# Spreading row norm factors through DRAM by two DMAs in a two-mixer decoder

## The chip, the cores and the metric

The kernel runs on one core of one Trainium2 chip. The metric is the device time of one execution in microseconds (us); lower is better. The profile is of one execution, taken by the hardware profiler.

## The reference

Two decoder layers work on 528 tokens (16 learned ones and the sequence of 512) with 1024 channels. Each layer is a half-step SwiGLU, a mixer and another half-step SwiGLU; layer 0 mixes by retention, layer 1 by gated linear attention (GLA), each with four heads. Both mixers end in the same way, and the change lies there:

```python
def rmsnorm(x, g):
    y = x * lax.rsqrt(jnp.mean(x * x, axis=-1, keepdims=True) + EPS)
    return y * g

# retention: 4 heads of 512 values     # gla: 4 heads of 256 values
o = rmsnorm(from_chunks(o), head_norm)
o = o.reshape(b, T, HEADS * DV) * jax.nn.silu(g)
return o @ w_out
```

So each token has, in each head, one factor 1/sqrt(mean square + EPS), by which all of the head's values are multiplied.

## The kernel before

**Layout.** Activations lie with channels on the partitions and tokens along the free axis. A retention head's output is four tiles of 128 x 528, a GLA head's two of 128 x 512 (the 16 learned tokens aren't needed any more there). A token's mean square is therefore a sum over partitions and tiles, and its factor must then stand on all 128 partitions.

**Products.** Every float32 product is three (`mm3`, L398 to L400): the high part of the weights by the high part of the data, the low by the high, the high by the low. A weight tile is loaded by a DMA into `raw` or `pair`, ScalarE casts it to its high half (`whi`, L159), and VectorE subtracts for the low half (`wlo`, L160). Projections go in "units", a 2 x 2 scheme of block products with seven steps (a11, s1, s2, a12, s3, s4, a22). A step of `rqk` (q or k of a retention head) is 12 products of 128 x 264. The steps sum into the PSUM tiles X and QZ; the results are put together by VectorE and ScalarE (for q and k: `row1` L1124, `c22` L1127, `c21` L1130), the first into tile 0, the others into tile 1 of `rtq` or `rtk`. The last step, a22, adds into X again and so has to wait until c22 has read X.

**What sets the order.** Each engine runs its own instructions in the order in which the scheduler put them, and that follows the program's order with some steps marked as urgent. After every step of a unit `hook` prepares further weights and counts down a queue of small jobs, `later(n, fn)`: the job at the head runs after n hooks. So the norm's parts are laid between steps of the next head's q and k units.

**The norm factors** (`rsqrt_rows`, L434). ScalarE squares the head's tiles and VectorE adds them up into `osq` (GLA: `gs`). TensorE multiplies each column block of 88 (GLA: 128) tokens, as weights, by one column of ones: `st`, with tokens on the partitions and a column per block (L443). VectorE scales it (`ms`, L446), GpSimd raises it to the power -1/2 (`r`, L448). VectorE multiplies `r` into blocks of the identity (`dg`, L450), and TensorE multiplies ones by `dg` (L456), which puts each token's factor on all partitions, in the PSUM tile `bc`: two products of 264 for a retention head, one of 512 for a GLA head. Each of these is float32, without the split in three. Then `finish` runs: in retention VectorE multiplies (L1335, half-width, eight of them), ScalarE casts the high part `ogh` (L431) and VectorE subtracts for the low part `ogl` (L432).

**Around the change.** In retention, head h's q unit, rotation (L1136 to L1145, `raq`, `rbq`, `rtq`, and the results `q`) and k unit are followed by `out(h - 1)`, the output projection of the head before (`po_r`), which reads `ogh` and `ogl`; values (`Xrv`), scores, gates (`gs0` to `gs3`) and the head's own products (`po`) come after. In GLA the heads are worked in pairs p = 0, 1 with j = 0, 1; the fourth's sums stand beside the output projection of the first pair. Behind head (1, 0) four tiles of the residual, spilled to DRAM earlier, are loaded again on SyncE's queue (L1937, 528 KB each).

Of the kernel before, what the change touches and what calls it, by code (L numbers as in the profile page):

```python
# [217 lines left out]
def trunk(ctx, tc, a):  # L218
# [163 lines left out]
    def later(n, fn):  # L382
        pend.append([n, fn])
# [50 lines left out]
    def rsqrt_rows(sq, parts, width, name, finish):  # L434


        n = sq.shape[1]
        np_ = n // parts
        w = 88 if n % 264 == 0 else 128
        nj = n // w  # L440
        st = bank(f"st_{name}")
        for j in range(nj):
            nc.tensor.matmul(st[:w, j:j + 1], lhsT=sq[:, j * w:(j + 1) * w], rhs=ones[:, 0:1],  # L443
                             start=(j == 0), stop=(j == nj - 1), skip_group_check=True)
# [3 lines left out]
        G.tensor_tensor(r[:w, :nj], ms[:w, :nj], half_neg[:w, :nj], ALU.pow)  # L448
        dg = tmp.tile([P, T], F32, tag="hf", name=f"dg_{name}")
        V.tensor_tensor(dg[:w, :n].rearrange("p (j t) -> p j t", j=nj),  # L450
                        ident[:w, :w].unsqueeze(1).broadcast_to([w, nj, w]),
                        r[:w, :nj].unsqueeze(2).broadcast_to([w, nj, w]), ALU.mult)

        def spread(q):
            bc = bank(f"bc_{name}{q}")
            nc.tensor.matmul(bc[:, :np_], lhsT=ones[:w, :], rhs=dg[:w, q * np_:(q + 1) * np_], start=True, stop=True)  # L456
            finish(bc, q)

        return [lambda q=q: spread(q) for q in range(parts)]

    def enter(gcol, by, lag=1, lag2=1):

# [90 lines left out]
    def pair(t, halves):  # L553

        return t[:, halves[0][0]:halves[1][1]].rearrange("p (b t) -> p b t", b=2)
# [516 lines left out]
    def retention(feed):  # L1072
        with tc.tile_pool(name="retp", bufs=1) as rp, tc.tile_pool(name="wmore", bufs=2) as wp, psum_pool(4) as pp:
# [40 lines left out]
            def head(h):  # L1114
                qk = {}

                def rope_pair(s):


                    t = [(rp if s == "k" else tmp).tile([P, T], F32, tag=f"gs{m}" if s == "k" else "sg",  # L1120
                                                        name=f"rt{s}{h}{m}") for m in range(2)]

                    def row1(ab, qz):
                        V.tensor_add(pair(t[0], HALVES), ab, qz)  # L1124

                    def c22(c, s_):
                        V.tensor_add(t[1][:, b0:b1], c, s_)  # L1127

                    def c21(c):
                        S.copy(t[1][:, a0:a1], c)  # L1130
# [189 lines left out]
                if h < RH - 1:  # L1320
# [20 lines left out]

# [31 lines left out]
    def gla(feed):  # L1373
        with tc.tile_pool(name="glap", bufs=1) as gp, psum_pool(2) as pp, \
# [448 lines left out]
            def pv(p, j):  # L1823
# [11 lines left out]
                            n == 0, False)  # L1835
                    nc.tensor.matmul(po[:, m, :], lhsT=vh[:3 * MR, 0, c], rhs=pr["PM"][:, j, :], start=False, stop=True)
# [4 lines left out]
                S.activation(s1[:, :512], po[:, 0, :], AF.Square)  # L1841
# [6 lines left out]
                def fin(bc, _):  # L1848
                    for m in range(2):
                        t = tmp.tile([P, 528], F32, tag="hf", name=f"gt{h}{m}")  # L1850
                        V.tensor_mul(t[:, :512], ob[:, m, :], bc)
# [8 lines left out]
                        split(oh[:, NM:], ol[:, NM:], t[:, :512])  # L1860
                        pr["og"][j, m] = (oh, ol)

                pr.setdefault("og", {})
                return lambda: rsqrt_rows(s1[:, :512], 1, 256, f"go{h}", fin)[0]

            def run(steps):
                for st in steps:
# [45 lines left out]
            renorm()  # L1913

            other["banks"], other["ring"] = 0, collections.deque(("bank0",))
            st = pv(0, 0)
            run(g[-n:4 - n])
            sp = st()
            run(g[4 - n:])
            sp()  # L1920
# [12 lines left out]
            sp = st()  # L1933
            run(g[n + 4:])
            for k in range(4):
                xs[k] = stream(k)
                nc.sync.dma_start(xs[k], spilt[k])  # L1937
            x[:] = [xs[d % 4][:, d // 4, :] for d in range(KD)]
            sp()
            st = pv(1, 1)  # L1940
            other["banks"], other["ring"] = 2, collections.deque(("bank0", "bank1"))
            out_step(0)
            sp = st()
            out_step(1)
            sp()
            out_step(2)
            out_step(3)
# [99 lines left out]
```

## Time and profile before

| | us |
|---|---|
| median of 3 runs | 2074.59 (2074.48 to 2075.45) |
| the profiled execution: span | 2072.5 |
| TensorE busy | 2061.5 (99%) |
| VectorE busy | 1789.9 (86%) |
| ScalarE busy | 1192.8 (58%) |
| GpSimd busy | 209.3 (10%) |

The span runs from the first to the last instruction of the profiled execution. Matmuls are pipelined, so that the start of one less the start of the one before, and not its own duration, says what it occupies. In rows of the timeline the columns are start, duration, engine, line, operation, output and inputs, shapes, and how many records are grouped; at the end may stand the idle time before and what ended it. Float32 products show two records each, with one weight load each.

### The profile page before, as it was taken

What the parts mean: (1) busy time and instruction counts of PE and PEld (TensorE: products, weight loads), DVE (VectorE), ACT (ScalarE), POOL (GpSimd) and SP (SyncE); (2) the same over time, 40 slices, a digit from 0 to 9 for tenths busy, and PEclk for the clock granted to TensorE, in tenths of its full rate; (3) what the DMA queues carried; (4) which work ended last, traced back from release to release, by engine and by line L of the source; (5) the groups of instructions that cost most, each with busy time, mean ns of one, the idle gap of its engine ahead of it and who ended that gap; (6) DMA issues with size and microseconds to landing.
All of it is one profiled execution on the core that took longest, in us unless ns stands there. A gap on an engine that the chain in (4) does not pass through costs nothing. (4 is left out here: it accounts for less than half of the span.)

```text
span 2072.5 us, 42971 instructions
## 1 busy us (share of the span) xinstructions
PE 2061.5 (99%) x16367; PEld 2016.6 (97%) x16367; DVE 1789.9 (86%) x3214; ACT 1192.8 (58%) x2330; POOL 209.3 (10%) x181
## 2 busy tenths in 40 slices
PE   9999999999999999999999999999999999999998
PEld 9999999999999999999999999999999988999998
DVE  8989889968686879988889998889997968998886
ACT  5656566554545455656566565666655445666664
POOL 1011111010101000111111011110101000111110
PEclk9999999999999999999999999999999999999999
DMA  7676767354554531776776376676614341686762
GB/s 223 159 190 162 193 179 193 98 144 132 144 133 131 142 101 67 183 188 161 187 194 179 107 180 181 151 208 172 200 57 117 93 162 60 166 210 175 183 178 72
DMA packets 176111, 318.84 MB, mean 154 GB/s; under 512 B 17568, under 2 KB 40736, under 8 KB 175904
## 3 DMA queue, kind: packets, MB, share of 16 engines
q1 hardware_dynamic: 133856, 237.04, 34.0%
q0 software_dynamic: 40896, 75.51, 22.4%
q10 hardware_dynamic: 1152, 3.55, 0.5%
q8 instruction: 128, 2.10, 0.4%
q14 instruction: 79, 0.65, 0.1%
HBM read 311.76 MB, written 4.26 MB: 152 GB/s over the span
## 5 line engine op out<-in xcount | busy, mean ns | idle before, releaser
L159 ACT CAST whi<-raw 128x512 fp32r<-128x512 f32 (+1 forms) x893 | 526.0, 606 | 484.3 <-DVE raw L165 97.3
L160 DVE TENSOR_TENSOR wlo<-raw,whi 128x512 fp32r<-128x512 f32 (+1 forms) x893 | 583.8, 669 | 143.4 <-ACT whi L159 136.1
L159 ACT CAST whi<-pair 128x512 fp32r<-128x512 f32 (+1 forms) x304 | 183.5, 604 | 119.5 <-PE Xf11u L399 7.3
L160 DVE TENSOR_TENSOR wlo<-pair,whi 128x512 fp32r<-128x512 f32 (+1 forms) x304 | 202.0, 665 | 7.0 <-ACT whi L159 5.6
L128 POOL DMA_DIRECT2D pair<-in_f_in x73 | 88.5, 1213 | 720.7 <-DVE wlo L160 338.7
L165 DVE TENSOR_TENSOR raw<-pair,raw 128x512 f32<-128x512 f32 (+1 forms) x146 | 97.3, 667 | 2.6
L167 DVE TENSOR_TENSOR raw<-raw,raw 128x512 f32<-128x512 f32 (+1 forms) x146 | 97.2, 666 | 2.4
L128 POOL DMA_DIRECT2D pair<-in_f_out x44 | 53.2, 1208 | 380.4 <-DVE wlo L160 133.6
L399 PE MATMUL po_r<-ogl,whi 128*128 128x264 f32 x256 | 72.7, 284 | 0.0
L398 PE MATMUL po_r<-ogh,whi 128*128 128x264 f32 x256 | 72.6, 283 | 0.0
L400 PE MATMUL po_r<-ogh,wlo 128*128 128x264 f32 x256 | 72.5, 283 | 0.0
L128 POOL DMA_DIRECT2D pair<-in_ret_in x20 | 24.3, 1216 | 297.2 <-DVE wlo L160 144.3
L398 PE MATMUL Xf20o<-hf,whi 128*128 128x264 f32 x176 | 50.9, 289 | 0.2
L398 PE MATMUL Xf11o<-hf,whi 128*128 128x264 f32 x176 | 50.9, 289 | 0.2
L398 PE MATMUL Xf10o<-hf,whi 128*128 128x264 f32 x176 | 50.8, 289 | 0.2
L399 PE MATMUL Xf10o<-hf,whi 128*128 128x264 f32 x176 | 50.0, 284 | 0.0
L399 PE MATMUL Xf11o<-hf,whi 128*128 128x264 f32 x176 | 50.0, 284 | 0.0
L399 PE MATMUL Xf20o<-hf,whi 128*128 128x264 f32 x176 | 50.0, 284 | 0.0
L400 PE MATMUL Xf20o<-hf,wlo 128*128 128x264 f32 x176 | 49.9, 285 | 0.0
L400 PE MATMUL Xf11o<-hf,wlo 128*128 128x264 f32 x176 | 49.9, 285 | 0.0
L400 PE MATMUL Xf10o<-hf,wlo 128*128 128x264 f32 x176 | 49.9, 285 | 0.0
L400 PEld LDWEIGHTS po_r<-ogh,wlo 128*128 128x128 f32 x256 | 48.2, 188 | 0.0
(987 smaller groups left out, 8523.9 us busy)
## 6 DMA issues: line engine op xcount, KB each, us to landing
raw<-in_f_in SPq DMA_DIRECT2D x277, 256.0 KB, 4.4
pair<-in_f_in SPq DMA_DIRECT2D x150, 256.0 KB, 4.7
pair<-in_f_in POOLq DMA_DIRECT2D x73, 512.0 KB, 6.4
raw<-in_f_out SPq DMA_DIRECT2D x80, 256.0 KB, 3.7
raw<-in_ret_in SPq DMA_DIRECT2D x76, 256.0 KB, 3.0
raw<-in_f_out SPq DMA_DIRECT2D x72, 192.0 KB, 3.0
pair<-in_f_out SPq DMA_DIRECT2D x48, 256.0 KB, 3.8
pair<-in_f_out POOLq DMA_DIRECT2D x24, 512.0 KB, 5.8
```

The costliest lines, as they stand in the source:

```text
L128: nc.gpsimd.dma_start(t, aps[2].unsqueeze(1).broadcast_to([P, 2, n]), accum_op=ALU.add)
L159: self.nc.scalar.copy(hi[:, :n], raw)
L160: V.tensor_sub(lo[:, :n], raw, hi[:, :n].bitcast(F32))
L165: V.tensor_add(s2, self.tiles[c][:, 1], self.tiles[c, "a11"])
L167: V.tensor_add(raw, raw, s2)
L398: nc.tensor.matmul(ps, lhsT=lh, rhs=rh, start=start, stop=False, **kw)
L399: nc.tensor.matmul(ps, lhsT=lh, rhs=rl, start=False, stop=False, **kw)
L400: return nc.tensor.matmul(ps, lhsT=ll, rhs=rh, start=False, stop=stop, **kw)
```

## The change

Retention heads 0, 1, 2 and all four GLA heads use a new function `rsqrt_sent`; retention head 3 and the norms between the blocks keep `rsqrt_rows`. The new function is four steps that the caller spaces out with `in_turn`:

- stats: the column sums as before, but the columns of one product are every sixth (GLA: fourth) token, so that the factors of consecutive tokens lie side by side on a partition; then scaling and power as before.
- send: a DMA on ScalarE's queue writes the 88 x 6 (GLA: 128 x 4) factors to a row in DRAM.
- fetch: a DMA on the same queue reads this row for each of the 128 partitions into an SBUF tile: the tile of the sums (`osq`, `gs1`) itself, or for the first head of a GLA pair a tile of its own, `gbc`.
- finish: the products with the factors, now full-width and in place (`gs0` to `gs3`, `gob`), and the split.

The tiles of k's rotation, which share buffers with the gate tiles, are now claimed when first written. The diff, cut to its core:

```diff
+    rows = ctx.enter_context(tc.tile_pool(name="rows", bufs=2, space=bass.MemoryType.DRAM))
...
+    def rsqrt_sent(sq, width, name, finish, into=None):
+        n = sq.shape[1]
+        w = 88 if n % 264 == 0 else P
+        nj = n // w
+        row = rows.tile([w, nj], F32, tag="row", name=f"row_{name}")
...
+                nc.tensor.matmul(st[:w, j:j + 1], lhsT=sq.rearrange("p (r j) -> p j r", j=nj)[:, j, :], rhs=ones[:, 0:1],
+                                 start=(j == 0), stop=(j == nj - 1), skip_group_check=True)
...
+        def send():
+            nc.scalar.dma_start(row, hold["r"][:w, :nj])
+
+        def fetch():
+            hold["bc"] = into() if into else sq
+            nc.scalar.dma_start(hold["bc"], row.rearrange("r j -> (r j)").unsqueeze(0).broadcast_to([P, n]))
+
+        return stats, send, fetch, lambda: finish(hold["bc"])
...
                     def row1(ab, qz):
-                        V.tensor_add(pair(t[0], HALVES), ab, qz)
+                        V.tensor_add(pair(place(0), HALVES), ab, qz)
...
-                    def fin(bc, q0, q1):
+                    def fin(bc):
                         for m in range(4):
-                            t = tmp.tile([P, T], F32, tag="hf", name=f"og{h}{m}{q0}")[:, :q1 - q0]
-                            V.tensor_mul(t, sgs[m][:, q0:q1], bc[:, :q1 - q0])
-                            split(og[h][0][m][:, q0:q1], og[h][1][m][:, q0:q1], t)
-
-                    later(2, lambda: stats(sqs, fin))
+                            V.tensor_mul(sgs[m], sgs[m], bc)
+                            split(og[h][0][m], og[h][1][m], sgs[m])
+
+                    in_turn((2, 2, 2, 3), rsqrt_sent(sqs, RDV, f"ro{h}", fin))
...
-                ob = gp.tile([P, 2, 512], F32, tag="Pd", name=f"gob{h}")
+                ob = gp.tile([P, 2, 512], F32, tag="Pd" if j else "Q", name=f"gob{h}")
...
-                        V.tensor_mul(t[:, :512], ob[:, m, :], bc)
+                        V.tensor_mul(ob[:, m, :], ob[:, m, :], bc)
...
+                return rsqrt_sent(s1[:, :512], 256, f"go{h}", fin, None if j else into)
...
-            st = pv(0, 1)
-            later(3, lambda st=st: later(3, st()))
+            fetch()
+            chain = pv(0, 1)
+            fin()
+            in_turn((3, 2, 2, 3), chain)
...
-            st = pv(1, 0)
+            stats, send, fetch, fin = pv(1, 0)
             run(g[n:n + 4])
-            sp = st()
-            run(g[n + 4:])
+            stats()
+            run(g[n + 4:n + 6])
+            send()
+            run(g[n + 6:])
+            fetch()
...
+            chain = pv(1, 1)
+            fin()
+            in_turn((1, 1, 1, 2), chain)
```

Lines of the changed kernel stand a little lower: L398 to L400 become L399 to L401, L1124 and L1127 become L1165 and L1168, L1136 to L1145 become L1177 to L1186; the head products are L1375, send and fetch L482 and L486. The scheduler's order changes with it, as the next pieces show (numbers behind names count tiles).

VectorE, in retention's second head, while its k unit runs and the first head is finished. Before, the head products (`og`, from `bc_ro`) and their low parts (`ogl`) stand around k's combine (`rtk11`), with q's rotation behind them:

```order
L432 TENSOR_TENSOR ogl0_6071<-og00264_6244,ogh0_6070 128x264
L160 TENSOR_TENSOR wlo274_6352<-raw138_6145,whi274_6351 128x512
L1127 TENSOR_TENSOR rtk11_6278<-Xrqkk1_6279,surqkk1_6281 128x264
L432 TENSOR_TENSOR ogl0_6071<-og01264_6248,ogh0_6070 128x264
L1335 TENSOR_TENSOR og02264_6252<-gs02_5834,bc_ro01_6242 128x264
L1335 TENSOR_TENSOR og03264_6256<-gs03_5835,bc_ro01_6242 128x264
L1124 TENSOR_TENSOR rtk10_6277<-surqkk1_6281,QZrqkk1_6280 128x528
L432 TENSOR_TENSOR ogl0_6071<-og02264_6252,ogh0_6070 128x264
L432 TENSOR_TENSOR ogl0_6071<-og03264_6256,ogh0_6070 128x264
L1136 TENSOR_TENSOR raq1_6261<-rtq10_6076,ropeq1_6072 128x528
L1138 TENSOR_TENSOR rbq1_6262<-rtq11_6077,ropeq1_6072 128x528
L1137 TENSOR_TENSOR rtq10_6076<-rtq10_6076,ropeq1_6072 128x528
```

The same place in the changed order:

```order
L1185 TENSOR_TENSOR rtq10_6203<-rtq10_6203,rtq11_6182 128x528
L1186 TENSOR_TENSOR q10_1_6235<-raq1_6228,q00_1_6234 128x528
L1375 TENSOR_TENSOR gs00_5699<-gs00_5699,osq0_5973 128x528
L433 TENSOR_TENSOR q11_1_6237<-rtq10_6203,q01_1_6236 128x528
L1375 TENSOR_TENSOR gs01_5700<-gs01_5700,osq0_5973 128x528
L433 TENSOR_TENSOR ogl0_6073<-gs00_5699,ogh0_6072 128x528
L1375 TENSOR_TENSOR gs02_5836<-gs02_5836,osq0_5973 128x528
L1165 TENSOR_TENSOR rtk10_6372<-surqkk1_6246,QZrqkk1_6245 128x528
L433 TENSOR_TENSOR ogl0_6073<-gs01_5700,ogh0_6072 128x528
L433 TENSOR_TENSOR ogl0_6073<-gs02_5836,ogh0_6072 128x528
L1168 TENSOR_TENSOR rtk11_6352<-Xrqkk1_6244,surqkk1_6246 128x264
L1375 TENSOR_TENSOR gs03_5837<-gs03_5837,osq0_5973 128x528
```

q's rotation has moved ahead of the head products, and k's combine `rtk11` behind most of them and behind `rtk10`.

TensorE at the end of the same k unit. Before, a22 into `Xrqkk1` ends and the out-projection `po_r00` begins:

```order
L400 MATMUL Xrqkk1_6279<-rth_4954,wlo269_6196 128x264
L398 MATMUL Xrqkk1_6279<-rth_4954,whi269_6195 128x264
L399 MATMUL Xrqkk1_6279<-rtl_4955,whi269_6195 128x264
L400 MATMUL Xrqkk1_6279<-rth_4954,wlo269_6196 128x264
L398 MATMUL po_r00_6430<-ogh0_6070,whi270_6232 128x264
L399 MATMUL po_r00_6430<-ogl0_6071,whi270_6232 128x264
L400 MATMUL po_r00_6430<-ogh0_6070,wlo270_6233 128x264
```

In the changed order, `po_r` and two of the values' first products follow s4 (`QZrqkk1`):

```order
L401 MATMUL QZrqkk1_6245<-uha_133,wlo268_6177 128x264
L399 MATMUL po_r00_6409<-ogh0_6072,whi270_6217 128x264
L400 MATMUL po_r00_6409<-ogl0_6073,whi270_6217 128x264
L401 MATMUL po_r00_6409<-ogh0_6072,wlo270_6218 128x264
L399 MATMUL po_r00_6409<-ogh0_6072,whi270_6217 128x264
L399 MATMUL Xrv10_6664<-uha_133,whi278_6422 128x264
L400 MATMUL Xrv10_6664<-ula_134,whi278_6422 128x264
L399 MATMUL po_r01_6440<-ogh0_6072,whi271_6259 128x264
L400 MATMUL po_r01_6440<-ogl0_6073,whi271_6259 128x264
L401 MATMUL po_r01_6440<-ogh0_6072,wlo271_6260 128x264
L399 MATMUL po_r01_6440<-ogh0_6072,whi271_6259 128x264
L400 MATMUL po_r00_6409<-ogl0_6073,whi270_6217 128x264
```

The 12 products of a22 into `Xrqkk1` now stand behind 19 products that were behind them, and the first read of the fourth tile's `ogl` comes 15 products after a22 begins. The third head has the same order; at the fourth head two products of `po_r` precede a22.

ScalarE, in the same head's q and k units, where the send and the fetch stand in the changed order among the weight casts (`rtq11` and `surqkk1` are copies of unit results):

```order
L159 CAST whi266_6139<-raw132_5755 128x512
L159 CAST whi267_6159<-pair51_5488 128x512
L482 DMA row_ro0_6074<-r_ro0_6124 88x6
L159 CAST whi268_6176<-raw132_5755 128x512
L159 CAST whi269_6196<-raw133_5790 128x512
L486 DMA osq0_5973<-row_ro0_6074 128x528
L1171 COPY rtq11_6182<-Xrqkq1_6079 128x264
L159 CAST whi270_6217<-raw134_5810 128x512
L159 CAST whi271_6259<-raw135_5892 128x512
L649 COPY surqkk1_6246<-Xrqkk1_6244 128x264
```

Two casts stand between send and fetch; before, there was no DMA in this place. In GLA, ScalarE's order now has the third head's fetch and its two casts ahead of the squares of the fourth head.

More of the change, by code (lines that the diff above doesn't have):

```diff
@@ L459, in rsqrt_rows, with stats, in_turn, step @@
         return [lambda q=q: spread(q) for q in range(parts)]
+    def rsqrt_sent(sq, width, name, finish, into=None):
[3 more added lines that the diff above has]
+        row = rows.tile([w, nj], F32, tag="row", name=f"row_{name}")
+        hold = {}
+        def stats():
+            st = bank(f"st_{name}")
+            for j in range(nj):
+                nc.tensor.matmul(st[:w, j:j + 1], lhsT=sq.rearrange("p (r j) -> p j r", j=nj)[:, j, :], rhs=ones[:, 0:1],
+                                 start=(j == 0), stop=(j == nj - 1), skip_group_check=True)
+            ms = tmp.tile([P, 8], F32, tag="ms", name=f"ms_{name}")
+            V.tensor_scalar(ms[:w, :nj], st[:w, :nj], 1.0 / width, EPS, ALU.mult, ALU.add)
+            r = hold["r"] = tmp.tile([P, 8], F32, tag="r", name=f"r_{name}")
+            G.tensor_tensor(r[:w, :nj], ms[:w, :nj], half_neg[:w, :nj], ALU.pow)
+        def send():
[4 more added lines that the diff above has]
+        return stats, send, fetch, lambda: finish(hold["bc"])
+    def in_turn(lags, steps):
+        def step():
+            steps[0]()
+            if steps[1:]:
+                in_turn(lags[1:], steps[1:])
+        later(lags[0], step)
     def enter(gcol, by, lag=1, lag2=1):
@@ L1915, in gla @@
             other["banks"], other["ring"] = 0, collections.deque(("bank0",))
-            st = pv(0, 0)
+            stats, send, fetch, fin = pv(0, 0)
             run(g[-n:4 - n])
-            sp = st()
-            run(g[4 - n:])
-            sp()
-            st = pv(0, 1)
-            later(3, lambda st=st: later(3, st()))
+            stats()
+            run(g[4 - n:6 - n])
+            send()
+            run(g[6 - n:])
+            fetch()
+            chain = pv(0, 1)
+            fin()
+            in_turn((3, 2, 2, 3), chain)
             for kind in ("gq", "gk"):
@@ L1930, in gla @@
             run(queue)
-            st = pv(1, 0)
+            stats, send, fetch, fin = pv(1, 0)
             run(g[n:n + 4])
-            sp = st()
-            run(g[n + 4:])
+            stats()
+            run(g[n + 4:n + 6])
+            send()
+            run(g[n + 6:])
+            fetch()
             for k in range(4):
@@ L1938, in gla @@
             x[:] = [xs[d % 4][:, d // 4, :] for d in range(KD)]
-            sp()
-            st = pv(1, 1)
+            chain = pv(1, 1)
+            fin()
+            in_turn((1, 1, 1, 2), chain)
             other["banks"], other["ring"] = 2, collections.deque(("bank0", "bank1"))
[L1942 to L1947, printed above, removed]
+            for dp in range(4):
+                out_step(dp)
             og = pairs[1]["og"]
```

17 lines of the change are left out of this document (10 added, 7 removed).

## The prediction

> **What bounds the kernel now.** I read the page first, then TensorE's waits around the change, then the stretch itself in the timeline.
>
> ```profile
> span 2072.5 us, 42971 instructions
> PE 2061.5 (99%) x16367; PEld 2016.6 (97%) x16367; DVE 1789.9 (86%) x3214; ACT 1192.8 (58%) x2330; POOL 209.3 (10%) x181
> PEclk9999999999999999999999999999999999999999
> ...
> PE po L398 <- DVE pl L432: 0.2, 1, 0.2
> ...
> 440.00:470.00 30.00, 30.00 (x242) 29.75 (x243) 23.37 (x48) 16.32 (x37) 2.96 (x2) 1.00 0.50 142
> ```
>
> TensorE is busy 2061.5 of 2072.5 us at full clock. The wait row is one of the two longest between 440 and 760 us, where the three retention heads stand: 0.2 us in 320. The last row is the window around the first of them (busy us of TensorE, its weight loads, VectorE, ScalarE, GpSimd, then the clock, the DMA share and GB/s): TensorE has no gap. So a product taken off TensorE shortens the span by what it occupies there, unless TensorE then waits for something that was in time before. I count against the span of 2072.5; the median of 2074.59 lies 2.1 us above it, and I add that at the end.
>
> **What goes from TensorE.**
>
> ```profile
> L456 PE MATMUL bc_ro<-dg_ro,ones x16: 383/386/435, 452.9 to 746.1; 88*128 88x264 f32 x16
> L456 PE MATMUL bc_go<-dg_go,ones x8: 592/592/592, 1576.2 to 1689.6; 128*128 128x512 f32 x8
> ...
> 451.47 0.28 PE L398 MATMUL QZrqkq<-uha,whi 128*128 128x264 f32 x1
> ...
> 452.92 0.66 PE L456 MATMUL bc_ro<-dg_ro,ones 88*128 88x264 f32 x2
> ...
> 454.87 0.61 PE L456 MATMUL bc_ro<-dg_ro,ones 88*128 88x264 f32 x2
> ...
> 456.79 0.28 PE L398 MATMUL QZrqkk<-rth,whi 128*128 128x264 f32 x1
> ...
> 1576.21 1.02 PE L456 MATMUL bc_go<-dg_go,ones 128*128 128x512 f32 x2
> 1577.30 0.40 PE L399 MATMUL go<-PF,v 128*128 128x512 f32 x1
> 1577.54 0.39 PE L400 MATMUL go<-PF,v 128*128 128x512 f32 x1
> ```
>
> Each spread is two records; starts are what counts, since matmuls overlap. A unit's step of 12 products takes 452.92 - 451.47 = 1.45 us (0.121 each). With a spread ahead of it a step takes 454.87 - 452.92 = 1.95 and 456.79 - 454.87 = 1.92, so the two spreads of a head cost 0.50 + 0.47 = 0.97 us: 2.9 for three heads. A GLA spread and one product of 512 together take 1577.30 - 1576.21 = 1.09, and such a product alone 0.24, so a spread is 0.85, and four are 3.4. The sum is 6.3 us off TensorE.
>
> **What is added off TensorE.** VectorE loses the diagonal and half of the short multiplies and subtractions: per retention head 0.62 and eight pairs of 0.34 for four pairs of 0.62, about 1.1 us less. VectorE isn't what ends the span, so I price this at nothing; its cover is TensorE's unbroken work. The factors now travel by two ScalarE-queue DMAs.
>
> ```profile
> L448 POOL TENSOR_TENSOR r_ro<-ms_ro,half_neg x4: 1645/1709/1730, 450.3 to 740.0; 88x6 f32<-88x6 f32 x4
> ...
> out<-endl SPq DMA_DIRECT2D x2, 128.0 KB, 1.8
> ...
> raw<-in_ret_in SPq DMA_DIRECT2D x76, 256.0 KB, 3.0
> ...
> ropeq<-in_rope ACTq DMA_DIRECT2D x3, 528.0 KB, 4.4
> ...
> x<-spill SPq DMA_DIRECT2D x4, 528.0 KB, 6.6
> ```
>
> No row shows a write of 2 KB or a broadcast read. The nearest write to DRAM lands in 1.8 us, the nearest reads of the fetch's size (264 KB) in 3.0, and 4.4 for twice that. The power ends about 450.3 + 1.7 = 452.1, the send lands at 454, and the fetch at 457 to 458.5. In the changed order VectorE comes to the first product with the factors some 13 operations of about 0.61 (rows below) after 453.33, at about 461.3: hidden, with some 3 us to spare. Sends and fetches stand in ScalarE's own sequence, so weight casts behind one wait with it: the send waits for the power, the fetch for the send. I price that at nothing, since ScalarE is busy 16.32 of the window's 30 us and its casts run ahead of TensorE; if that lead is used up, each us of lateness reaches TensorE. The later placing of k's tiles, the products in place, the other buffer for a GLA head's product and the plain loop over the out steps add no instruction: nothing.
>
> **What moves, in retention.** Two moves stand in the order: on VectorE q's rotation now precedes the head products, and they the last combine of k; on TensorE the out-projection's first products precede k's last step (a22), which waits for that combine.
>
> ```profile
> 453.33 0.69 DVE L1124 TENSOR_TENSOR rtq<-surqkq,QZrqkq 128x528 f32<-128x528 f32 x1
> ...
> 462.34 0.69 DVE L160 TENSOR_TENSOR wlo<-raw,whi 128x512 fp32r<-128x512 f32 x1
> 462.94 0.43 DVE L1127 TENSOR_TENSOR rtk<-Xrqkk,surqkk 128x264 f32<-128x264 f32 x1
> 463.29 0.43 DVE L432 TENSOR_TENSOR ogl<-og,ogh 128x264 fp32r<-128x264 f32 x1
> ...
> 466.33 0.70 DVE L1138 TENSOR_TENSOR rbq<-rtq,ropeq 128x528 f32<-128x528 f32 x1
> 466.95 0.70 DVE L1137 TENSOR_TENSOR rtq<-rtq,ropeq 128x528 f32<-128x528 f32 x1
> ...
> 464.08 0.29 PE L398 MATMUL Xrqkk<-rth,whi 128*128 128x264 f32 x1
> ```
>
> From starts: a weight half takes 0.60, a half-wide combine 0.35, a full-wide operation 0.62. VectorE's q combine starts at 453.33, held by TensorE, so it stays there. In the changed order 22 operations run from it to k's combine, seven of 0.60, one of 0.35 and fourteen of 0.62: 13.2 us, to 466.55. Four more of 0.62 bring the last head product's low half: 469.0. TensorE would be at the moved block at 464.08 - 0.97 = 463.11; 19 products stand ahead of a22, so it comes there at 465.4 and waits 1.1 us; 15 products on, at 468.4, it reads that low half and waits 0.6. That is 1.8 us for the first head, and the second has the same order: 3.6.
>
> The third is followed by a different order.
>
> ```profile
> 660.42 0.70 DVE L450 TENSOR_TENSOR dg_ro<-ident,r_ro 88x528 f32<-88x528 f32 x1 [1.24 <-POOL r_ro L448]
> 661.05 0.42 DVE L1127 TENSOR_TENSOR rtq<-Xrqkq,surqkq 128x264 f32<-128x264 f32 x1
> ...
> 662.59 0.69 DVE L1124 TENSOR_TENSOR rtq<-surqkq,QZrqkq 128x528 f32<-128x528 f32 x1
> ...
> 672.68 0.28 PE L398 MATMUL Xrqkk<-rth,whi 128*128 128x264 f32 x1
> ```
>
> Without the diagonal's 0.63 q's combine starts at 661.96; 17 operations (10.5 us) and the combine (0.35) stand to 672.8. TensorE, with two moved products ahead of a22, is there at 672.68 - 0.97 + 0.24 = 671.95 and waits 0.85; the weight half read 14 products later ends four operations after the combine, 675.2, against 674.5. Together 1.5. Here the first product with the factors stands sixth after the combine, so the fetch has no slack. Retention's waits come to 5.1 us, with ends of 0 (VectorE's operations fall back into the gaps that I don't see) and 8 (casts late as well).
>
> **What moves, in the second mixer.**
>
> ```profile
> 1671.42 2.15 SPq L1937 DMA_DIRECT2D x<-spill  x4
> ...
> 1673.44 1.28 DVE L1851 TENSOR_TENSOR gt<-gob,bc_go 128x512 f32<-128x512 f32 x2
> ...
> 1677.34 0.60 ACT L1841 ACTIVATE gs<-go 128x512 f32<-128x512 f32 x1 [1.96 <-PE go L1836]
> ```
>
> The first, second and fourth heads have several steps between send, fetch and use: nothing. The third's fetch meets four 528 KB reloads issued from 1671.42 on. In the changed order ScalarE's two casts of that head's result, which wait for the fetch, stand ahead of the fourth head's squares, which TensorE's next column sums need. A fetch of 3.0 us from 1671.5 gives casts until about 1677, as late as the square started before; one that takes the reloads' 6.6 is 3.6 later. I take 0.8, nearer the first end, since the fetch writes half of one reload's bytes, with ends 0 and 3.6.
>
> **Strided column sums.** The products with one column of ones now load their 88 or 128 weight columns with a step of six or four numbers, to make each partition's factors consecutive.
>
> ```profile
> 449.03 1.03 PE L443 MATMUL st_ro<-ones,osq 128*88 128x1 f32 x12
> 449.92 0.37 PE L398 MATMUL Xrqkq<-rth,whi 128*128 128x264 f32 x1
> ...
> 1570.88 0.95 PE L443 MATMUL st_go<-ones,gs 128*128 128x1 f32 x8
> 1571.69 0.37 PE L398 MATMUL Xgg<-gth,whi 128*128 128x264 f32 x1
> ```
>
> They take 0.89 and 0.81 us now, 3 x 0.89 + 4 x 0.81 = 5.9 in all. No row shows a strided load. The ends are nothing and a doubling, 5.9. I take nothing: a load with its product takes 0.89 / 12 = 74 ns for 88 columns, which is about 1.2 a ns, whereas the moving side reads 264 in 121 ns, 2.2 a ns, so the load is not at the speed of the reads. The Trainium skill, "SBUF — State Buffer", section "Door 1: The DMA port swizzle", speaks against this: lines there are 16 bytes and every access that crosses to a new line pays a penalty, so steps of 24 and 16 bytes would pay at each column. By that rule, priced as a doubling (my estimate), the sum below would be 5.9 higher; no row here shows it.
>
> The sum: 2072.5 - 6.3 + 5.1 + 0.8 = 2072.1 us of span, with 2.1 outside 2074.2. From a measurement of this kernel 0.2%, 4.1 us, can be told from no change.
>
> **Rivals.**
> (A) *The waits don't come.* I summed VectorE's operations from 453.33 on without regard to work done before that point; if weight halves are made earlier, as a VectorE with less to do allows, the 5.9 us of waits shrink to some 1.5. For it: only 23.37 of 30 us of VectorE were busy in the window, and the change takes work from it. Against: from 453.33 to 469 it had hardly a gap already. Time: 2074.6 - 6.3 + 1.5 = 2069.8.
> (B) *Strided weight loads double.* Place: the seven column sums; price 5.9, all on TensorE. It decides for slower once a load costs about 1.8 times its present time (2078.7 is 4.5 above the forecast, and 4.5 of 5.9 is 0.76). Time 2074.2 + 5.9 = 2080.1. For it: nothing hides TensorE; against: the two rates above.
> (C) *The DMAs land late.* The fetch reads one row for all 128 partitions while some 142 GB/s of weights stream. If it takes 6.6 us like the reloads rather than 3.0, the third head, with no slack, and the third GLA head lose about 3 us each where I took at most 0.8: 2074.2 + 5 = 2079.
> That the change does not do what it says is excluded: the spread products are gone from the order for all seven heads.
>
> **How the numbers follow.** Forecast (the sum, between 2070.5 and 2078.7): 0.52. A: 0.26. B: 0.11. C: 0.11. A lies mostly under 2070.4, the bound of faster; a little of it stays within: faster 0.25, same 0.54, slower 0.21 (B and C, short of a little). The range takes in A at 2069.8 with retention's lower end, and B: 2068.8 to 2080.0, some 0.8.
>
> **What would show it.** Right: spread groups of only four records (the last retention head), and waits of TensorE for k's combine and the head products' low half at about 465 and 468 us, near 1.1 and 0.6, the like a head later; the send and fetch landing in 1.8 and 3 to 4.4 us; column sums in 0.89 and 0.81 us. A shows if these waits are under 0.3; B if column sums take over 1.5 us a head; C if the fetch lands after VectorE reaches its product, and VectorE is idle there. I am wrong altogether if TensorE waits where neither move stands.

## The result and the profile after

The changed kernel takes 2101.94 us (2100.08 to 2103.95) against 2074.53: a ratio of 1.0131 with an interval of 1.0119 to 1.0143. It is slower by 27 us and lies far above the range, which ended at 2080.0. The spread products are gone as the order said. The first lines of the page, and TensorE's waits over the whole kernel (total us, times, longest):

```profile
span 2098.3 us, 42914 instructions
PE 2070.5 (99%) x16347; PEld 2024.3 (96%) x16347; DVE 1785.2 (85%) x3183; ACT 1191.6 (57%) x2318; POOL 210.3 (10%) x181
...
PE st_go L474 <- DVE gs L1886: 6.8, 1, 6.8
PE Xrqkk L399 <- ACT surqkk L653: 3.6, 3, 1.5
PE Xgq L399 <- ACT gssggq L649: 2.1, 1, 2.1
PE Xrqkk L399 <- DVE rtk L1168: 1.5, 1, 1.5
PE po_r L400 <- DVE ogl L433: 1.5, 4, 0.5
PE Xgk L399 <- ACT gssggk L649: 1.2, 1, 1.2
```

TensorE is busy 9 us longer although it has fewer products, and idle 28 us instead of 11. So two questions stand: what made its own work longer, and what it waits for. For the first, the weight loads of the column sums, before (L443) and after (L474), and the clock in a stretch of GLA's first pair of heads and one of the second (after the busy times comes the clock granted to TensorE, as a share of full speed):

```profile
L443 PEld LDWEIGHTS st_ro<-ones,osq x48: 153/158/158, 448.9 to 739.4; 128*88 128x88 f32 x48
L443 PEld LDWEIGHTS st_go<-ones,gs x32: 187/192/192, 1570.8 to 1683.4; 128*128 128x128 f32 x32
...
L474 PEld LDWEIGHTS st_ro<-ones,osq x36: 233/248/248, 448.8 to 666.7; 128*88 128x88 f32 x36
L474 PEld LDWEIGHTS st_go<-ones,gs x32: 309/329/332, 1581.5 to 1704.9; 128*128 128x128 f32 x32
...
1595.00:1598.00 3.00, 0.85 (x7) 0.64 (x6) 2.71 (x5) 3.00 (x7) 0.00 (x0) 1.00 0.94 150
1598.00:1601.00 3.00, 3.00 (x18) 3.00 (x17) 2.37 (x4) 1.03 (x3) 0.00 (x0) 0.58 0.10 18
1601.00:1604.00 3.00, 3.00 (x15) 3.00 (x16) 0.76 (x2) 0.26 (x2) 1.40 (x1) 0.50 0.05 6
1604.00:1607.00 3.00, 3.00 (x21) 3.00 (x21) 2.11 (x4) 1.06 (x2) 0.00 (x0) 0.78 0.05 8
...
1702.00:1705.00 3.00, 1.68 (x8) 1.71 (x8) 1.78 (x3) 0.00 (x0) 0.00 (x0) 0.50 0.00 0
1705.00:1708.00 3.00, 3.00 (x9) 2.44 (x10) 0.80 (x2) 0.00 (x0) 1.42 (x1) 0.50 0.21 66
1708.00:1711.00 3.00, 3.00 (x9) 2.35 (x8) 1.29 (x2) 0.62 (x1) 0.00 (x0) 0.50 0.19 44
```

A weight load with a step took 248 ns where the plain one takes 158, and 329 against 192. And with the gaps of 2.15 and 6.8 us in GLA the clock went to half, for 6.8 and 10.2 us; behind the gap of 1.2 us it stayed at full. In the profile of before it left full only in the last 2.5 us of the span. For the second question, the first GLA pair in ScalarE's, VectorE's and TensorE's timelines:

```profile
1588.24 0.35 ACTq L486 DMA_DIRECT2D gbc<-row_go  x1
...
1594.31 1.22 ACT L432 CAST gohl<-gob 128x512 fp32r<-128x512 f32 x2 [4.28 <-DVE gob L1890]
1595.44 0.59 ACT L1881 ACTIVATE gs<-go 128x512 f32<-128x512 f32 x1
1595.93 0.59 ACT L1882 ACTIVATE gs<-go 128x512 f32<-128x512 f32 x1
1596.41 0.62 ACT L159 CAST whi<-raw 128x512 fp32r<-128x512 f32 x1
1596.92 0.39 ACT L649 COPY gssggq<-Xgq 128x264 f32<-128x264 f32 x1
...
1593.59 1.29 DVE L1890 TENSOR_TENSOR gob<-gob,gbc 128x512 f32<-128x512 f32 x2 [2.83 <-DMA gbc<-row_go]
...
1597.36 0.39 PE L399 MATMUL Xgq<-gth,whi 128*128 128x264 f32 x1 [2.15 <-ACT gssggq L649]
```

The fetch was issued at 1588.24 and VectorE's product started at 1593.59, 5 us later. ScalarE stood 4.28 us at the casts of that product; the next head's squares, a weight cast and the copy of `Xgq` were behind them, and TensorE stood 2.15 us for that copy. In the second pair the fetch landed 7.1 us after its issue:

```profile
1691.08 0.33 ACTq L486 DMA_DIRECT2D gbc<-row_go  x1
...
1698.20 1.29 DVE L1890 TENSOR_TENSOR gob<-gob,gbc 128x512 f32<-128x512 f32 x2 [4.32 <-DMA gbc<-row_go]
...
1698.93 1.22 ACT L432 CAST gohl<-gob 128x512 fp32r<-128x512 f32 x2 [5.49 <-DVE gob L1890]
1700.05 0.59 ACT L1881 ACTIVATE gs<-go 128x512 f32<-128x512 f32 x1
...
1703.32 2.00 PE L474 MATMUL st_go<-ones,gs 128*128 128x1 f32 x8 [6.81 <-DVE gs L1886]
```

Here the squares of the fourth head stood 5.49 us behind the third's casts, and its column sums on TensorE 6.81. In the first two heads of retention TensorE waits (1.3 and 1.5 us) for copies that stand behind a weight cast, which itself waits 2.5 and 2.7 us for its weights; at the third, VectorE stands 1.8 us for the fetch, and TensorE then 0.8 for a copy and 1.5 for k's combine. ScalarE at the first head, then the fetch's issue to landing for the three (least, median, most):

```profile
461.45 0.62 ACT L159 CAST whi<-raw 128x512 fp32r<-128x512 f32 x1 [2.46 <-DMA raw<-in_ret_o]
461.97 0.37 ACT L653 COPY surqkk<-Xrqkk 128x264 f32<-128x264 f32 x1
...
DMA to landing us min/median/max: 5.0/5.4/5.7
```

By the first product of the values' third step in the second head (491.7 us before, 495.4 after) retention lost 3.7 us, and 11 in all by its last output product; GLA lost 15.

### The profile page after: what moved, and what is told of

The parts are those of the page before. It is cut to its first block, busy times and chain, and to the rows that moved or that the text cites. A ratio compares the mean times of both kernels' runs of the same rounds, so it can differ in the third digit from the quotient of the medians.

```text
span 2098.3 us, 42914 instructions
## 1 busy us (share of the span) xinstructions
PE 2070.5 (99%) x16347; PEld 2024.3 (96%) x16347; DVE 1785.2 (85%) x3183; ACT 1191.6 (57%) x2318; POOL 210.3 (10%) x181
## 4 chain that ended last, share of the span: by engine, by line
PE 66%; DVE 3%; DMA 2%; ACT 1%; issue 1%; POOL 0%; POOLq 0%; ACTq 0%; DVEq 0%
PE po_r L400 1%; PE po_r L401 1%; PE po_r L399 1%; PE Xf20o L399 1%; PE Xf20o L401 1%; PE Xf20o L400 1%; PE lv L1619 1%; PE Xf11u L399 1%; PE Xf21u L401 1%; PE Xf21o L399 1%; PE Xf21u L400 1%; PE Xf21u L399 1%; PE Xf11u L400 1%; PE Xf11u L401 1%; PE Xf20u L399 1%
## 5 line engine op out<-in xcount | busy, mean ns | idle before, releaser
L400 PE MATMUL po_r<-ogl,whi 128*128 128x264 f32 x256 | 73.2, 287 | 1.5 <-DVE ogl L433 1.5
L399 PE MATMUL po_r<-ogh,whi 128*128 128x264 f32 x256 | 72.9, 285 | 0.3 <-DVE rtk L1165 0.3
L401 PE MATMUL po_r<-ogh,wlo 128*128 128x264 f32 x256 | 72.5, 284 | 0.5 <-DVE wlo L160 0.5
L399 PE MATMUL Xf20o<-hf,whi 128*128 128x264 f32 x176 | 50.9, 289 | 0.2
L399 PE MATMUL Xf11o<-hf,whi 128*128 128x264 f32 x176 | 50.9, 289 | 0.2
L399 PE MATMUL Xf10o<-hf,whi 128*128 128x264 f32 x176 | 50.8, 288 | 0.2
L400 PEld LDWEIGHTS po_r<-ogl,whi 128*128 128x128 f32 x256 | 48.1, 188 | 2.4 <-DVE ogl L433 2.3
L400 PE MATMUL Xf20o<-hf,whi 128*128 128x264 f32 x176 | 50.0, 284 | 0.0
L400 PE MATMUL Xf11o<-hf,whi 128*128 128x264 f32 x176 | 50.0, 284 | 0.0
L400 PE MATMUL Xf10o<-hf,whi 128*128 128x264 f32 x176 | 50.0, 284 | 0.0
L401 PE MATMUL Xf20o<-hf,wlo 128*128 128x264 f32 x176 | 49.9, 285 | 0.0
L401 PE MATMUL Xf11o<-hf,wlo 128*128 128x264 f32 x176 | 49.9, 285 | 0.0
L401 PE MATMUL Xf10o<-hf,wlo 128*128 128x264 f32 x176 | 49.9, 284 | 0.0
```

Source lines behind the costliest of these rows:

```text
L399: nc.tensor.matmul(ps, lhsT=lh, rhs=rh, start=start, stop=False, **kw)
L400: nc.tensor.matmul(ps, lhsT=lh, rhs=rl, start=False, stop=False, **kw)
L401: return nc.tensor.matmul(ps, lhsT=ll, rhs=rh, start=False, stop=stop, **kw)
```

## The experiments

**Theory and rivals.** Theory: three things add up, and each is a consequence of the transfer, not of the missing products: strided weight loads; work in ScalarE's and VectorE's fixed order behind a fetch of 5 to 7 us; and a clock that falls behind the gaps. Rivals: the two halves disturb each other; the clock falls for another reason; retention's loss is its order alone, or the transfer's competition with weights alone.

**Plain columns.**

```diff
-  lhsT=sq.rearrange("p (r j) -> p j r", j=nj)[:, j, :]
+  lhsT=sq[:, j * w:(j + 1) * w]
```

> The changed kernel with one edit: the column sums of the sent norms take consecutive tokens as weight columns again, so that the factors land on the wrong tokens; every transfer, order and size stays. If the step between weight columns is what doubled the sums (1.89 and 1.91 us against 1.03 and 0.95), they fall back to about 0.89 and 0.81 us from start to next start and the time drops by 3 x 0.8 + 4 x 0.95 = 6 us or somewhat more, to about 2095. If the sums are long for another reason (ScalarE's transfers, a colder clock), they stay at 1.8 and the time at 2102.

In this version the factors come to stand at other tokens; the transfers, the order and the sizes stay. Measured: 2094.97 us against the changed kernel's 2101.94, 7.0 less (ratio to before 1.0098, interval 1.0083 to 1.0113). The loads are back:

```profile
L474 PEld LDWEIGHTS st_ro<-ones,osq x36: 154/158/158, 449.1 to 664.5; 128*88 128x88 f32 x36
L474 PEld LDWEIGHTS st_go<-ones,gs x32: 187/192/338, 1579.0 to 1699.3; 128*128 128x128 f32 x32
```

From start to the next product's start a head's sums take 0.89 us again, against 1.75. The step between columns costs 6 to 7 us: this part of the theory holds.

**Each half alone.** Retention's half is the changed kernel with GLA's part of the diff undone; GLA's half the reverse.

> Retention's half of the change alone; GLA as before. By landmarks in the two traces (the values' first product of head 2 at 491.7 and 495.4, the last output product at 781.4 and 792.5) retention costs 3.7 us a head, 11 in all: 2085.7. If the two halves disturb each other through shared pools and queues, it differs from that by over 2 us.

> GLA's half alone; retention as before. By landmarks GLA costs 5.6 us in the first pair of heads and 9.3 in the second, 15: 2089.5, with TensorE's granted clock at half for some 7 us in each pair. If the clock fell for another reason than the gaps in GLA (power, or the stretch before), it does not fall here and the time is about 2081.

Measured: retention's half 2086.98 us (ratio 1.0060, 1.0044 to 1.0077), 12.7 over before; GLA's half 2086.34 (1.0057, 1.0042 to 1.0072), 12.1 over. Together 24.8 of 27.4: the halves are nearly independent. What GLA's half lacks is in the first pair: it had gaps of 1.1 and 2.0 us there and no fall of the clock, where the changed kernel had gaps of 2.15 and 1.2 us and 6.8 us at half clock. Part of what I expected of it, half clock in each pair, did not come.

**GLA's products behind the next squares.**

```diff
-            fin()
-            in_turn((3, 2, 2, 3), chain)
+            later(2, behind_sum(0, fin))     # fin ordered after the next head's sum of squares
+            in_turn((1, 2, 2, 3), chain)
```

and likewise for the second pair.

> The changed kernel with one edit: in GLA the products with the fetched factors and their casts stand behind the next head's squares and their sum. The transfers stay and land as late as they do (5 and 7 us). If the loss in GLA is that ScalarE and VectorE stand at the late fetch with the squares behind it, TensorE's waits of 2.1 and 6.8 us go, the clock stays at full, and the time falls by some 11 us (2.1 + 6.8, and half of the 6.9 and 9 us at half clock, less what new waits appear), to about 2090. If the late fetch itself holds TensorE (its buffers, or the weights it delays), the time stays above 2098.

Measured: 2086.61 us (1.0060, 1.0045 to 1.0075), 15.3 under the changed kernel, more than expected. TensorE's waits in GLA and the first window of GLA and that of the second pair:

```profile
PE Xgk L399 <- ACT gssggk L649: 0.4, 1, 0.4
PE st_go L474 <- DVE gs L1886: 0.3, 1, 0.3
...
1575.00:1615.00 40.00, 39.34 (x294) 38.38 (x293) 28.88 (x51) 19.91 (x40) 5.65 (x5) 1.00 0.52 124
1685.00:1715.00 30.00, 30.00 (x139) 25.25 (x139) 18.54 (x30) 10.17 (x18) 1.42 (x1) 1.00 0.52 177
```

The fetch still takes up to 6.8 us, but nothing that TensorE needs stands behind it, and in GLA the clock stays at full. The time is that of retention's half alone: GLA's loss was the order behind the fetch, not the fetch.

**Reloads behind the fetch.**

```diff
-                nc.sync.dma_start(xs[k], spilt[k])
+                nc.scalar.dma_start(xs[k], spilt[k])
```

> The changed kernel with one edit: the four reloads of 528 KB are issued on ScalarE's queue behind the fetch, not on SyncE's beside it. ScalarE's order changes a little with it: the fourth head's squares stand ahead of the third's casts. If the fetch of the third GLA head landed 7.1 us after its issue because the reloads shared the engines with it, it now lands in 3 to 4. If the weights alone or the row's broadcast are slow, it stays at 5 or above. TensorE's wait of 6.8 us and the half clock behind it go in either case as far as they come from the order of casts and squares: 2102 less about 10.

Measured: 2095.94 us (1.0101, 1.0086 to 1.0117). The third head's fetch lands after 4.8 us instead of 7.1, and TensorE's wait at the fourth head's sums is 1.1 instead of 6.8. So the reloads cost that fetch 2.3 us; the 4.8 that stay are not theirs. The order changed with the edit, so that the time does not divide between the two, and 6 us is less than the 10 expected: the first pair had gaps of 2.5 and 2.1 this time, and the clock fell twice for 3.4 us.

**A gap alone.** The kernel before, with five more powers behind the fourth head's:

```diff
+        for _ in range(5 if name == "go3" else 0):
+            G.tensor_tensor(r[:w, :nj], r[:w, :nj], ones[:w, :nj], ALU.pow)
```

> The kernel before, with no transfer added: the fourth GLA head's power is followed by five more powers with exponent one on GpSimd (about 1.4 us each, 7 us), so that its spread comes late and TensorE stands for some 3 to 4 us once. If a gap of TensorE alone halves the granted clock for a time, the clock shows 0.5 for several us behind the gap, and the time rises by the gap and some 3 us more: 2081. If the clock fell in the changed kernel for another reason (the transfers, the reloads), it stays at 1.00 and the time rises by the gap alone, to about 2078.

Measured: 2078.53 us (1.0019, 1.0009 to 1.0028), 3.8 over before. The gap came out shorter than the 3 to 4 us expected:

```profile
1692.11 1.10 PE L458 MATMUL bc_go<-dg_go,ones 128*128 128x512 f32 x2 [2.31 <-DVE dg_go L452]
...
1690.00:1700.00 10.00, 7.89 (x33) 6.14 (x34) 7.98 (x13) 2.62 (x5) 1.16 (x2) 1.00 0.23 76
1700.00:1710.00 10.00, 10.00 (x45) 8.18 (x44) 4.84 (x9) 3.15 (x6) 0.00 (x0) 1.00 0.30 96
```

After 2.31 us the clock stayed full. It does not show that a gap alone lowers the clock, nor that it doesn't; that stays with the rows of the other runs, below.

**No fetch in retention.** Retention's half without the line that reads the row back; the heads are multiplied by their column sums instead.

> Retention's half alone (2087.0) without the fetch: the factors' row is written but not read back, and the head is multiplied by its column sums instead of its factors. The order on TensorE and VectorE stays close to that of retention's half. If the fetch's 264 KB compete with the weights (DMA share 0.9 to 1.0 from 456 to 464 us, and a cast that waits 2.5 us for a weight tile, with the copy behind it that TensorE waits for, 4.5 us over three heads), these waits go and the time falls by 4 to 6 us, to about 2082. If the order alone is to blame, the time stays within 1.5 us of 2087.

Measured: 2084.79 us (1.0047, 1.0030 to 1.0064), 2.2 less. The waits for copies went (4.5 us in retention's half), but two of 2.6 and 2.3 for the weights of the early value products came in their place. Neither expectation was met as it stands. But each of the new waits was followed by 3.4 us at half clock, which the trace of retention's half has nowhere there. In such a stretch 18 products start instead of some 30, 0.12 us each: about 1.5 us lost, 3 for both. Without them the time would be some 5 us under retention's half (an estimate), in the 4 to 6 expected if the fetch competes with the weights. The clock fell here with no fetch in the kernel, so the fetch itself is not what lowers it.

**A buffer of its own for k's second tile.**

```diff
-  tag=f"gs{m}" if s == "k" else "sg"
+  tag=("gs0", "rk1")[m] if s == "k" else "sg"
```

> Retention's half alone with one edit: the second tile of k's rotation has a buffer of its own instead of the one of the second gate tile, which since the change is multiplied in place and read until its low half is made. VectorE's order then has k's combine ahead of three of the four head products, and TensorE's a22 stands ahead of the out-projection again, as before the change. If that shared buffer made the order and the order costs what I summed, TensorE's waits for the combine and the low halves (3.3 us by the list of waits, and some breaks between interleaved products) go: 5 us less, about 2082. If the loss is the fetch's competition with the weights, the time stays within 1.5 us of 2087.

Measured: 2084.76 us (1.0049, 1.0034 to 1.0064), 2.2 less. k's a22 stands ahead of the out-projection again, the 1.5 us for the combine are gone, but 3.8 us for copies behind late weights stay, and the clock fell once for 3.4 us (some 1.5 lost). So the order around a22 came from the shared buffer, and it was worth less than the 5 expected.

**Both.**

> Retention's half alone with both edits: k's second rotation tile in a buffer of its own, and no fetch (the heads are multiplied by their column sums). Each edit alone gave 2.2 us of 12.3, and in each a wait was left: with the fetch gone TensorE waited 2.6 and 2.3 us for the weights of two value products that stand early in the changed order, with the tile apart it waited 1.8 and 1.1 for copies behind late weights. If each edit only uncovered the other's wait, the two together give more than 4.4: with the strided sums (2.6) against the spreads saved (2.9), the time comes to 2075 to 2077. If a third cause carries the rest, it stays at 2081 or above.

Measured: 2083.60 us (1.0039, 1.0026 to 1.0053), 3.4 under retention's half. This refuted the pair of causes: 8.5 us were left. Its waits in retention name the next one, the first input of the out-projection:

```profile
PE po_r L399 <- ACT ogh L432: 2.6, 2, 1.3
PE Xrqkk L401 <- DVE wlo L160: 1.3, 1, 1.3
```

**The finish three hooks earlier.**

```diff
-  in_turn((2, 2, 2, 3), rsqrt_sent(sqs, RDV, f"ro{h}", fin))
+  in_turn((2, 2, 1, 1), rsqrt_sent(sqs, RDV, f"ro{h}", fin))
```

> Retention's half without the fetch and with the tile apart (2083.6), with one edit more: the waits in hooks between the four steps are 2, 2, 1, 1 instead of 2, 2, 2, 3, so that the head products are made three hooks earlier, ahead of q's rotation, as before the change. In the version without this edit TensorE still waited 1.3 us a head for the out-projection's first input and some 1.2 more in short stops; sums of starts put 2.7 us a head beyond before, 0.86 of it the strided sums. If the late finish is the third cause, the stops go and what stays is the strided sums less the spreads: within 1 us of 2075. If not, it stays at 2082 or above.

> The version with the early finish, no fetch and the tile apart, and the column sums taken over consecutive tokens as well. It leaves of retention's change only the send, the missing spreads and the longer, fewer products with the factors: if the account is closed, this is faster than before by the spreads, 2 to 3 us: 2072 to 2073, and 2.6 under the version with strided sums. If the strided loads cost nothing where TensorE no longer waits, it equals that version.

> As retention's half with the tile apart (2084.8), fetch and right factors included, with the steps 2, 2, 1, 1 hooks apart: the head products stand ahead of q's rotation again, but the fetch takes 5.4 us from issue to landing, some 3.7 steps of 1.45 us, where the order now gives it about one. If VectorE and ScalarE stand at the fetch with weight halves behind them, TensorE waits 2 us or more a head and the time stays at 2084 or rises; the transfer's own latency then is what kept the finish late. If the weights ahead cover it, it falls to 2080 or below, and the late finish was only a choice of lags.

The first two have no fetch and k's second tile apart, the third has the fetch. Measured: early finish without fetch 2076.80 us (1.0008, 0.9998 to 1.0017), 6.8 less than with the late one (which also has one fall of the clock, some 1.5 of it); with plain columns too 2074.50 (0.9998, 0.9989 to 1.0008); early finish with the fetch 2079.38 (1.0024, 1.0015 to 1.0034), 5.4 less than with the late one. The late finish was the largest single part of retention's loss. The list of waits of the first of the three shows what is left in retention, at the third head:

```profile
PE Xrqkk L401 <- DVE wlo L160: 1.2, 1, 1.2
PE QZrqkk L401 <- DVE wlo L160: 0.3, 1, 0.3
```

The strided sums are 2.3 us of what is left (2076.80 less 2074.50; 3 x 0.86 by the trace). With plain columns too, I expected 2072 to 2073 and got 2074.5. From one head's column sums to the next's, the first two heads now take 103.2 us where they took 104.17 and 104.16: the spreads' 0.97 each is there. The third takes 82.6 where it took 81.3, these 1.5 us of waits included, and so most of the gain is lost again. The version with the fetch is 2.6 us over its twin without, and the fetch was given one hook where it takes 5.4 us; its waits are again for ScalarE's copies (3.8 us), behind transfers. So the lags of the change were no necessity: with one buffer more for k's tile and an earlier finish retention's half comes from 2086.98 to 2079.38.

**A faster version.** Retention as before; GLA sent, the finish behind the next squares, plain weight columns. For the factors to come out in the order of the tokens, first the squares were written out of order, then VectorE's sum of them read out of order:

```diff
-  V.tensor_add(s1[:, :512], s1[:, :512], s2[:, :512])
+  V.tensor_add(s0[:, :512].rearrange("p (j r) -> p j r", j=4),
+               *(t[:, :512].rearrange("p (r j) -> p j r", j=4) for t in (s1, s2)))
```

> A version meant to be faster than both: retention as before; GLA sent by DMAs, the products with the factors behind the next head's squares, and the squares written by ScalarE in such an order that the column sums take weight columns side by side while the factors still come out in the order of the tokens. What is left of the change's account is then the four spread products, 3.4 us less than before: 2070.9. If ScalarE's scattered writes cost much (four writes of 0.6 us in the way), or the late fetch still holds TensorE, it is 2074 or more.

> As the version whose squares were written out of order (2073.0; its squares took 1.13 us each instead of 0.60, and TensorE waited 1.3 us once for their sum), with one edit: the squares are written plainly and VectorE's one sum of them reads out of order. If VectorE reads with a step of 16 bytes at its usual pace (0.68), the waiting and the longer squares go, and the time is 2071.5, 3 us under before. If VectorE is slower at it too (1.3 or so), it stays at 2073.

Measured: squares out of order 2073.05 us (0.9993, 0.9983 to 1.0002), the sum out of order 2071.30 (0.9982, 0.9973 to 0.9990), 3.8 under before (2075.13 beside it) and about the 3.4 of the four spreads. VectorE is slower with a step, but only once a head, and TensorE's wait shrinks to 0.7:

```profile
L1884 DVE TENSOR_TENSOR gs<-gs,gs x4: 1074/1088/1089, 1568.2 to 1679.9; 128x512 f32<-128x512 f32 x4
...
PE st_go L474 <- DVE gs L1884: 0.7, 1, 0.7
```

It beats both kernels: the idea of the change holds for GLA where its three costs are avoided.

## Why the prediction was wrong

**What held.** TensorE bounds the kernel, and the spreads were worth about what I summed: 3.8 us in GLA's faster version against 3.4, 0.96 a head against 0.97 in the first two heads of retention. Of the waits in the moved order, the one for the head products' low half came in the first two heads (0.5 us each, 0.6 taken), and the one for k's combine behind the third (1.5, 0.85 taken). The combine of the first two, 1.1 taken for each, did not hold TensorE.

**Strided column sums: priced at nothing, measured 6 to 7 us.** I took the rate of the moving side (2.2 numbers a ns) as a sign of room. The loads took 248 and 329 ns with steps of 24 and 16 bytes against 158 and 192. The Trainium skill, "SBUF — State Buffer", section "Door 1: The DMA port swizzle", which says that each access that crosses to a new 16-byte line pays, agrees with these rows: the weight loads took 57% and 71% longer and the sums about twice their time, close to the 5.9 that I had put beside it.

**The fetch: 3 to 4.4 us taken, 5.0 to 5.7 measured in retention, 5.3 and 7.1 at the first heads of GLA's pairs** (3.9 and 3.7 at the second heads). The slack of 3 us in VectorE's order was there for the first retention head, so that the late landing itself cost nothing there; at the third, where I had seen no slack, VectorE stood 1.8 us. What the first two could not take was the competition: the DMA share from 456 to 464 us was 0.81 already before, and a weight tile that comes later holds ScalarE and what stands behind. The run without the fetch, where these waits are gone, speaks for this.

**GLA: 0.8 us taken, 15 measured.** This is the step that failed most, and the place was named: the third head's casts ahead of the fourth's squares. I had an end of 3.6 for it and took the near one; the wait was 6.8. For the first head I wrote that several steps lay between, without looking at what ScalarE's order put behind its casts: the same squares, and a copy that TensorE needs (2.15 us, and 1.2 later). The waits come to 10.1 us; with the strided sums (some 3.9), less the spreads (3.4), and with the clock (below), that is about the 15. The run with the products behind the squares gives back 15.3.

**The clock was not in the sum.** The gaps of 2.15 and 6.8 us cost their own length and then a stretch at half clock: 6.8 us in the first pair, 7.8 behind the gap in the second. The column sums within these stretches took no longer (1.69 and 1.86 us from start to next start, 1.78 at full clock), the rest not quite twice its time: some 5 of the 15 us, by an estimate.

**Retention: 5.1 taken, 12.7 measured.** I took the order as given and priced its waits one by one. In the runs that take the causes out one after another, the finish three hooks later is 6.8 us of it, the shared buffer and the fetch 3.4 together, the strided sums 2.3 to 2.6. The parts depend on that order: the fetch alone is 2.2 beside the late finish and shared buffer, 1.2 with the buffer apart, 2.6 beside the early finish; and in three of these versions (no fetch, the buffer apart, both) the clock fell as well.

**The rivals were not alternatives.** B came in full, A did not. C came in its sign, the late landing; in GLA it cost far more than its 3 us, since I had priced the lateness of the transfer and not what stands behind it. I gave each a chance for itself, so that the range ended at 2080; their costs add, and they make gaps for the clock to fall in.

## What to carry to other kernels

Taking 6 us off a busy TensorE is worth 6 only if what replaces it puts no wait of some microseconds ahead of anything that TensorE needs in another engine's fixed order; list, for each new wait, what stands behind it on that engine. A wait that opens a gap of more than about a microsecond on TensorE may bring 3.4 us or a multiple of it at half clock, and is priced with that. And an access with a step is priced as slower until a row shows otherwise.

## What the runs showed of the hardware

The clock fell behind shorter gaps than I would have thought, and not always. A gap of 2.50 us brought a fall in the run with plain columns and none in the run with the reloads behind the fetch:

```profile
1607.63 0.39 PE L399 MATMUL Xgk<-gth,whi 128*128 128x264 f32 x1 [2.50 <-ACT gssggk L649]
...
1605.19:1608.61 3.42, 0.98 (x8) 0.98 (x9) 3.30 (x6) 2.60 (x6) 1.24 (x1) 1.00 0.40 149
1608.61:1612.02 3.41, 3.41 (x18) 3.41 (x17) 1.51 (x3) 0.90 (x2) 0.00 (x0) 0.50 0.83 141
...
1598.22 0.39 PE L399 MATMUL Xgq<-gth,whi 128*128 128x264 f32 x1 [2.50 <-ACT gssggq L649]
...
1593.59:1597.00 3.41, 2.14 (x18) 1.92 (x16) 2.46 (x4) 1.82 (x4) 1.25 (x1) 1.00 0.59 135
1597.00:1600.41 3.41, 2.19 (x16) 2.19 (x16) 3.12 (x6) 2.35 (x6) 0.00 (x0) 1.00 0.56 97
```

The windows are not chosen freely. The stretches at half clock within a trace start and end on a grid of 3.413 us: in the changed kernel at 1598.50, 1605.34, 1700.90 and 1711.14, that is 0, 2, 30 and 33 steps from the first. In the first run almost all of the gap lies within one step, in which TensorE is busy 0.98 us; in the second a step's border cuts it, and both steps have over 2 us of work. So it goes in the other traces: eight steps with a gap and 0.81 to 1.66 us of work were followed by one at half clock, and steps with a gap and 1.71 us or more (the gap alone, 2.31 us long, left 1.71) were not. There are two exceptions: a step with 1.56 us in GLA's half had no fall, and one with 2.31 us, a gap of 1.09 and column sums, had one. Where column sums fell into a step at half clock, the next was at half too (both pairs of the changed kernel); that they count as little work would fit, but no run tests it. So the place of a gap on this grid counts beside its length. The Trainium skill, "TensorE: Matmul & The Clock Gate", section "Why this matters for your kernels", advises to avoid idle gaps over about 3 us; here gaps of 1.76 to 2.61 us were enough seven times.

ScalarE's squares written with a step of 512 bytes took 1.13 us instead of 0.60, VectorE's sum read with a step of 16 bytes 1.09 instead of 0.68. In the changed kernel a broadcast read of 2 KB to 128 partitions took 3.7 to 7.1 us from issue to landing, a write of 2 KB 1.4 to 4.9.
